# A mixture-of-experts block: the second expert's rows fetched early, and four slot tables in place of sixteen

## The chip, the cores and the metric

The kernel runs on one core of a Trainium2 chip. The metric is device time in microseconds (us), the median of the runs shown. The engines are PE (TensorE), DVE (VectorE), ACT (ScalarE), POOL (GpSimd) and SP (SyncE, which here only issues transfers). Line numbers (L1545) are those of the kernel before.

## The reference

Two transformer blocks over 512 tokens of 1024 features. The first is a sparse-attention mixer and a dense MLP; the second is differential attention with a pooling mixer, a mixture of experts, and a small gated term. The change lies in the routing of the mixture of experts:

```python
logits = xt @ w_router + b_router                 # 512 tokens x 32 experts
top_vals, top_idx = lax.top_k(logits, 4)
gates = softmax(top_vals)
...
for each expert e, over the tokens that chose it:
    gt = minimum(x @ w_gate[e] + b_gate[e], 7)
    up = clip(x @ w_up[e] + b_up[e], -7, 7)
    y  = ((up + 1) * gt * sigmoid(1.702 * gt)) @ w_down[e] + b_down[e]
out[token] += gate * y
```

where `xt` is the RMS-normed residual. The 32 experts' weights are three matrices of 1024 x 1024 in float32 each, 4 MB apiece, and each is read once from HBM.

## The kernel before

**Experts.** The last half of the program goes through 32 places. A place is an expert with room for a fixed number of its tokens: 112 for the places that are not in `FEW`, 64 for those that are. The first three places (`STATIC`) are experts 0 to 2; the others are experts in the order of how many tokens chose them, so that their numbers are known only at run time. `seq` lists the work as 768 parts, a part being 128 rows of one weight matrix: gate and up of place 0, gate and up of place 1, down of place 0, gate and up of place 2, and so on. `begin[p]` is the index of the first part of place p: 0, 16, 40, 64 for the first four.

**Parts.** float32 products are made from float32r halves. `fetch` (L1539) loads two parts with one DMA of 1 MB on SP's queue (L1545) into one of ten buffers taken in turn (`units`); ACT writes the high half `whi` of a part and DVE the low half `wlo` (both L297, the helper `split`). A buffer is free for the next load when both of its parts are split. The halves go to slots of a ring of 17 tiles (14 named s0 to s13, then `x0`, `x1` and `e0`, listed at L837), two for each part, which PE frees when it has used them. `product` (L1723) multiplies a part by the place's rows: six matmuls for a place of 112 rows, four for one of 64.

**Order.** PE, DVE, ACT and POOL run their instructions of this stretch in the order in which the program lists them (`in_order`, L1987). SP's loads are issued in program order, each when its waits are over. In the main loop (L1972), turn i first fetches up to part i + 6, then runs what `put(i, ...)` has laid beside it, then does the product of part i.

**Rows.** The rows of place p are fetched from HBM by an indirect DMA that POOL issues (`gather`, L1498) into the one buffer `xg`, transposed on PE (`turn_rows`, L1793) and split (`split_rows`, into `he` for place 0 and `xe` for the others). Place 0's are fetched from `base`, the residual before the norm, and scaled by their norms in the buffer (L1655); the other places' are fetched from `normed`, the residual after the norm, which ACT's queue stores tile by tile (`store_normed`, L1404). Place 1's gather (L1970) stands behind five of the scatters below; its `turn_rows` is beside part 10 and its `split_rows` beside part 11.

**Which rows.** For places 0 and 1 (and 2, inside the loop) the list of rows comes from a one-hot matrix product (`one_hot`, `slot_products`, `tokens_of`); for place 1 this stands at L1650 to L1653, behind the work that ranks the experts (`ranks`, `places`). For the places from 3 on it comes from tables in HBM: `scatter_entries` (L1576) writes, by 16 indirect DMAs of POOL, for each of the 512 x 4 choices of a token an entry of four numbers to row `place` of a table; there is one table for each of the four token tiles and four choices, cleared beforehand. `table_slots` (L1763) loads the 16 tables by ACT's queue beside parts 24 to 27, `sum_tables` (L1772) adds them on DVE beside parts 32 and 33, and `all_slots` (L1778) beside part 34 makes the row lists. An entry of zero is an empty slot, so a sum over tables merges them.

**`lower`** is a buffer of 128 x 1024 whose rows 0 to 63 are cleared by POOL (L1474); it is used from the first place in `FEW` on.

Of the kernel before, what the change touches and what calls it, by code (L numbers as in the profile page):

```python
# [10 lines left out]
F32 = mybir.dt.float32  # L11
# [228 lines left out]
def build(tc, I, out, dbg=None, stop=None):  # L240
# [3 lines left out]
    with es:  # L244
# [558 lines left out]
        def attention(g, fill):  # L803
# [7 lines left out]
            for i in range(len(units) + AHEAD):  # L811
# [4 lines left out]
                if i in fill:  # L816
# [20 lines left out]
                  {forward - 1: [f"g{i}" for i in range(3)], mixer - 1: [f"p{i}" for i in range(5)], experts - 1: ['x0', 'x1', 'e0']}, {"g": mixer - 1, "p": mixer + 3}, mixer)  # L837
# [434 lines left out]
        tables = [dram.tile([P * NE, 4], F32, name=f"table{j}") for j in range(4 * NT)]  # L1272
# [201 lines left out]
        nc.gpsimd.memset(lower[0:P - SMALL].bitcast(F32), 0.0)  # L1474
# [8 lines left out]
        slots = {}  # L1483

# [13 lines left out]
        def gather(p, src, m, ap):  # L1498
            nc.gpsimd.indirect_dma_start(out=xg[:m], out_offset=None, in_=src, in_offset=bass.IndirectOffsetOnAxis(ap=ap, axis=0),  # L1499
                                         bounds_check=S - 1, oob_is_err=False)  # L1500
# [75 lines left out]
        def scatter_entries(js):  # L1576
            for j in js:
                nc.gpsimd.indirect_dma_start(out=tables[j], out_offset=bass.IndirectOffsetOnAxis(ap=place[:, j // 4, j % 4:j % 4 + 1], axis=0), in_=entry[:, j // 4, j % 4], in_offset=None,
                                             bounds_check=P * NE - 1, oob_is_err=False)
# [45 lines left out]
        slot_products(ptok, oh0, (1, 2, 3), 4, told)  # L1625
        weigh(2)
# [6 lines left out]
        one_hot(slot_of[:, :, 0:1], (0,), oh0)  # L1633
        slot_products(ptok, oh0, (0,), 4, told)
        pn = W["rb"][:, 2 * NT]
        for t2 in range(NT):
            nc.tensor.matmul(pn, ones, chosen[:, t2], start=t2 == 0, stop=t2 == NT - 1)
        gi0 = tokens_of(ptok, 0)

        gather(0, base, CAP, gi0)  # L1640
        norm0 = early.tile([P, 4], F32, name="norm0")[:CAP]
        nc.vector.tensor_copy(norm0, ptok[:CAP, 0:4])
        nc.vector.tensor_tensor(out=norm0[:, 3:4], in0=norm0[:, 1:2], in1=norm0[:, 2:3], op=ALU.add)
# [6 lines left out]
        oh1, ptok1 = new_one_hot(), ps_tr(1)  # L1650
        one_hot(slot_of[:, :, 1:2], range(NT), oh1)
        slot_products(ptok1, oh1, range(NT), 2, [])
        gi1 = tokens_of(ptok1, 1)  # L1653
        fetch(2)
        for cs in (slice(0, 512), slice(512, D)):  # L1655
            scale_rows(xg[:CAP, cs], xg[:CAP, cs], norm0[:, 3:4], gpre[:CAP, cs])
# [106 lines left out]
        def table_slots(q):  # L1763

            if q == 0:
                sums.extend(row_tile("tabs").rearrange("p (j f) -> p j f", j=8) for _ in range(2))
            for j in range(4 * q, 4 * q + 4):
                nc.scalar.dma_start(sums[j // 8][:, j % 8], tables[j].rearrange("(s e) c -> s (e c)", e=NE))

        sums = []  # L1770

        def sum_tables(h):  # L1772
            tab = tabs[h] = row_tile("tab")[:, :4 * NE].rearrange("p (e c) -> p e c", c=4) if h else early.tile([P, NE, 4], F32, name="tab")
            nc.vector.reduce_sum(tab.rearrange("p e c -> p (e c)"), sums[h].rearrange("p j f -> p f j"), axis=AX)
# [3 lines left out]
        def all_slots():  # L1778
            tab = tabs[0]
            nc.vector.tensor_tensor(out=tab, in0=tab, in1=tabs[1], op=ALU.add)  # L1780
# [12 lines left out]
        def turn_rows(p):  # L1793
            pts["x", p] = turned(xg, cap[p])
# [124 lines left out]
        put(11, split_rows, 1)  # L1919
        put(14, gates_by_expert)  # L1920
# [6 lines left out]
        for q in range(4):  # L1927
            put(begin[1] + 8 + q, table_slots, q)
        for h in range(2):
            put(begin[1] + 16 + h, sum_tables, h)  # L1930
# [35 lines left out]
        scatter_entries(range(15, 10, -1))  # L1966
# [3 lines left out]
        gather(1, normed, CAP, gi1)  # L1970
# [307 lines left out]
```

## Time and profile before

| | |
|---|---|
| three runs | 2075.34, 2075.75 (median) and 2076.8 us |
| profiled execution | 2073.2 us |
| its span, first to last instruction | 2071.5 us |
| PE / DVE / ACT / POOL busy | 1968.3 / 1640.3 / 1370.9 / 414.6 us |
| moved by DMA | 554.16 MB, mean 268 GB/s |
| mean granted clock of PE, in shares of full speed | 0.985 |

Busy time counts what an engine executes; a matmul that is pipelined behind another counts as busy. The times of rows are microseconds from the start of the span. The experts' stretch runs from about 920 to 1980; its first matmul on an expert's weights starts at 928.86.

### The profile page before, as it was taken

Reading aid. Unit: us, or ns where it says so; the run is one execution under the profiler, and the core shown is the slowest. Engines: PE = TensorE matmul, PEld = TensorE weight load, DVE = VectorE, ACT = ScalarE, POOL = GpSimd, SP = SyncE. Lnnn points to the kernel's source line nnn. Section 1 sums busy time; section 2 is a strip of 40 time slices with the busy share of each in tenths; the row PEclk is TensorE's granted clock in tenths of the full one; section 3 lists DMA queues with packets and bytes.
Section 4 is the critical chain, followed back from the end, with each engine's and each line's share of the span. In section 5 each row is a group of like instructions: output and inputs, shape, how many; then the busy total and the mean of one; then the engine's idle time right before and its main releaser. Section 6 shows DMA issues by size and latency. Waiting matters only on the chain. (4 is left out here: it accounts for less than half of the span.)

```text
span 2071.5 us, 28687 instructions
## 1 busy us (share of the span) xinstructions
PE 1968.3 (95%) x9675; PEld 1507.0 (73%) x9676; DVE 1640.3 (79%) x2290; ACT 1370.9 (66%) x1889; POOL 414.6 (20%) x363
## 2 busy tenths in 40 slices
PE   8999999999999888878999999999999999999968
PEld 6777779888878887666777777777667766767546
DVE  6688874223466666678999999999999999999965
ACT  5656753222355364537799988888888888888942
POOL 0100120000010334124223444322211003201122
PEclk9999999999999998989999999999999999999989
DMA  5510464233555402248999999999999999999973
GB/s 215 173 31 22 176 230 154 91 102 102 182 202 191 129 11 72 107 173 338 403 410 406 412 406 407 402 404 402 405 396 403 399 398 402 398 407 398 365 270 106
DMA packets 113158, 554.16 MB, mean 268 GB/s; under 512 B 16739, under 2 KB 25955, under 8 KB 63852
## 3 DMA queue, kind: packets, MB, share of 16 engines
q1 hardware_dynamic: 90528, 510.04, 63.6%
q10 hardware_dynamic: 15116, 25.40, 3.6%
q0 software_dynamic: 7360, 16.82, 2.4%
q8 instruction: 78, 1.28, 0.2%
q14 instruction: 76, 0.62, 0.1%
HBM read 532.62 MB, written 26.66 MB: 270 GB/s over the span
## 5 line engine op out<-in xcount | busy, mean ns | idle before, releaser
L297 DVE TENSOR_TENSOR wlo<-wraw,whi 128x1024 fp32r<-128x1024 f32 x923 | 1076.1, 1215 | 209.4 <-ACT whi L297 203.8
L297 ACT CAST whi<-wraw 128x1024 fp32r<-128x1024 f32 x923 | 923.1, 1049 | 217.2 <-PE po L327 28.0
L1715 POOL DMA_INDIRECT ybuf<-yt,si x31 | 190.6, 6150 | 453.4 <-ACT yt L1820 453.4
L326 PE MATMUL pw<-whi,xe 128*112 128x512 f32 x544 | 215.9, 397 | 0.0
L327 PE MATMUL pw<-wlo,xe 128*112 128x512 f32 x544 | 214.4, 394 | 0.1
L328 PE MATMUL pw<-whi,xe 128*112 128x512 f32 x544 | 214.0, 393 | 0.0
L1734 PE MATMUL pw<-wlo,xe 128*64 128x512 f32 x406 | 162.9, 401 | 8.6 <-DVE wlo L297 8.0
L1733 PE MATMUL pw<-whi,xe 128*128 128x512 f32 x406 | 161.3, 397 | 3.2 <-DVE xe L297 3.2
L332 POOL TENSOR_SCALAR rstd<-ss 128x1 f32<-128x1 f32 (+1 forms) x68 | 24.8, 364 | 626.9 <-DVE ss L877 387.5
L326 PE MATMUL pw<-whi,he 128*112 128x512 f32 x320 | 128.1, 400 | 0.0
L1499 POOL DMA_INDIRECT xg<-normed,gi x31 | 62.5, 2017 | 327.2 <-PE tr L1703 284.8
L327 PE MATMUL pw<-wlo,he 128*112 128x512 f32 x320 | 126.4, 395 | 0.2
L328 PE MATMUL pw<-whi,he 128*112 128x512 f32 x320 | 126.2, 394 | 0.0
L328 PEld LDWEIGHTS pw<-whi,xe 128*112 128x112 f32 x544 | 94.7, 174 | 31.6
L326 PEld LDWEIGHTS pw<-whi,xe 128*112 128x112 f32 x544 | 94.7, 174 | 31.2
L327 PEld LDWEIGHTS pw<-wlo,xe 128*112 128x112 f32 x544 | 94.8, 174 | 30.9 <-DVE wlo L297 0.7
L1733 PEld LDWEIGHTS pw<-whi,xe 128*128 128x128 f32 x406 | 76.4, 188 | 34.2 <-DVE xe L297 3.6
L1734 PEld LDWEIGHTS pw<-wlo,xe 128*64 128x64 f32 x406 | 54.5, 134 | 46.4 <-DVE wlo L297 31.1
L1733 PE MATMUL pw<-whi,he 128*128 128x512 f32 x182 | 74.1, 407 | 0.0
L1734 PE MATMUL pw<-wlo,he 128*64 128x512 f32 x182 | 72.9, 401 | 0.0
L326 PE MATMUL pa<-x2T,whi 128*128 128x512 f32 (+1 forms) x200 | 72.6, 364 | 0.1
L327 PE MATMUL pa<-x2T,whi 128*128 128x512 f32 (+1 forms) x200 | 72.6, 363 | 0.0
(617 smaller groups left out, 4212.7 us busy)
## 6 DMA issues: line engine op xcount, KB each, us to landing
wraw<-in_we_gate_dram SPq DMA_DIRECT2D x128, 1024.0 KB, 20.4
wraw<-in_we_up_dram SPq DMA_DIRECT2D x128, 1024.0 KB, 21.5
wraw<-in_we_down_dram SPq DMA_DIRECT2D x128, 1024.0 KB, 20.4
wraw<-in_w_gu_dram SPq DMA_DIRECT2D x44, 512.0 KB, 3.8
wraw<-in_w_down_dram SPq DMA_DIRECT2D x44, 512.0 KB, 4.5
wraw<-in_w_out_dram SPq DMA_DIRECT2D x24, 512.0 KB, 5.6
yb<-ybuf SPq DMA_DIRECT2D x6, 1024.0 KB, 8.7
wraw<-in_w_v_dram SPq DMA_DIRECT2D x10, 512.0 KB, 3.9
```

What stands on the lines that cost most here:

```text
L297: return nc.scalar.copy(hi, src), nc.vector.tensor_tensor(out=lo, in0=src, in1=hi.bitcast(F32), op=ALU.subtract)
L326: nc.tensor.matmul(o, a[0], b[0], start=start, stop=False)
L327: nc.tensor.matmul(o, a[0], b[1], start=False, stop=False)
L328: W["mm"] = nc.tensor.matmul(o, a[1], b[0], start=False, stop=stop)
L332: ins = nc.gpsimd.tensor_scalar(out=r[:, :w], in0=ss, scalar1=1.0 / n, scalar2=eps, op0=ALU.mult, op1=ALU.add)
L1499: nc.gpsimd.indirect_dma_start(out=xg[:m], out_offset=None, in_=src, in_offset=bass.IndirectOffsetOnAxis(ap=ap, axis=0), bounds_check=S - ...
L1715: nc.gpsimd.indirect_dma_start(out=ybuf, out_offset=bass.IndirectOffsetOnAxis(ap=ap, axis=0), in_=y_, in_offset=None, bounds_check=4 * S - ...
L1733: nc.tensor.matmul(ps[:, cs], a[:, k, 0:P], hi, start=first, stop=False)
L1734: nc.tensor.matmul(ps[:m, cs], a[:, k, 0:m], lo, start=False, stop=False)
```

## The change

Place 1's rows are fetched next to place 0's, from `base`, into a buffer of their own: `x1`, in the tile that was the ring's 17th slot (`e0`), so that the ring has 16. For that the one-hot product for place 1 is made before the ranking of the experts, in the storage of `lower`, whose clearing moves into the loop (beside part 12). Both places' rows are scaled by their norms on DVE. All 16 scatters stand together ahead of the loop, and write to four tables, one for each choice, in place of 16. The four tables are loaded by POOL's queue beside part 20, and added by one reduction beside part 26.

```diff
@@ -834,7 +834,7 @@
         stages += ["ppppr"] + ["pp"] * 6 + ["pppp", "pppprr"]
         experts = len(stages)
         open_ring("ring2", stages + ["h"] * (NE * 24), lambda u: 2 if u < experts - 1 else SPLIT_AHEAD if u >= experts else 0,
-                  {forward - 1: [f"g{i}" for i in range(3)], mixer - 1: [f"p{i}" for i in range(5)], experts - 1: ['x0', 'x1', 'e0']}, {"g": mixer - 1, "p": mixer + 3}, mixer)
+                  {forward - 1: [f"g{i}" for i in range(3)], mixer - 1: [f"p{i}" for i in range(5)], experts - 1: ['x0', 'x1']}, {"g": mixer - 1, "p": mixer + 3}, mixer)
         if stop == "mix":
             with pool("dd") as dd:
                 for n, m in (("mixA", mixA), ("mixG", mixG)):
@@ -1269,7 +1269,7 @@
         normed = dram.tile([S, D], F32, name="normed")
         ybuf = dram.tile([4 * S, D], F32, name="ybuf")
 
-        tables = [dram.tile([P * NE, 4], F32, name=f"table{j}") for j in range(4 * NT)]
+        tables = [dram.tile([P * NE, 4], F32, name=f"table{j}") for j in range(4)]
         zeros = mixq.tile([P, 4 * NE], F32, name="zeros")
         nc.gpsimd.memset(zeros, 0.0)
         for t in tables:
@@ -1471,7 +1471,8 @@
         fold = early.tile([P, SMALL], F32R, name="fold")
         nc.vector.tensor_copy(fold, ident[:, P - SMALL:P])
         lower = early.tile([P, D], F32R, name="lower")
-        nc.gpsimd.memset(lower[0:P - SMALL].bitcast(F32), 0.0)
+        x1 = W["e0"].tile([P, D], F32, name="x1")
+        nc.gpsimd.memset(x1, 0.0)
         braws = [xg[0:NE]] + [raw_tile()[0:NE] for _ in range(2)]
         for braw, n in zip(braws, ("gate", "up", "down")):
             nc.sync.dma_start(braw, I["be_" + n])
@@ -1482,6 +1483,9 @@
             nc.vector.tensor_copy(pick0[64 * q:64 * q + 64, q], eye[64 * q:64 * q + 64, 0:STATIC])
         slots = {}
 
+        def fetched(p):
+            return x1 if p == 1 else xg
+
         def one_hot(col, tiles, oh):
             n = len(tiles)
             t = slice(tiles[0], tiles[0] + n)
@@ -1496,7 +1500,7 @@
                 done.append(tt)
 
         def gather(p, src, m, ap):
-            nc.gpsimd.indirect_dma_start(out=xg[:m], out_offset=None, in_=src, in_offset=bass.IndirectOffsetOnAxis(ap=ap, axis=0),
+            nc.gpsimd.indirect_dma_start(out=fetched(p)[:m], out_offset=None, in_=src, in_offset=bass.IndirectOffsetOnAxis(ap=ap, axis=0),
                                          bounds_check=S - 1, oob_is_err=False)
 
         def tokens_of(pt, p):
@@ -1575,7 +1579,7 @@
 
         def scatter_entries(js):
             for j in js:
-                nc.gpsimd.indirect_dma_start(out=tables[j], out_offset=bass.IndirectOffsetOnAxis(ap=place[:, j // 4, j % 4:j % 4 + 1], axis=0), in_=entry[:, j // 4, j % 4], in_offset=None,
+                nc.gpsimd.indirect_dma_start(out=tables[j % 4], out_offset=bass.IndirectOffsetOnAxis(ap=place[:, j // 4, j % 4:j % 4 + 1], axis=0), in_=entry[:, j // 4, j % 4], in_offset=None,
                                              bounds_check=P * NE - 1, oob_is_err=False)
 
 
@@ -1623,6 +1627,9 @@
         oh0, ptok, told = new_one_hot(), ps_tr(0), []
         one_hot(slot_of[:, :, 0:1], (1, 2, 3), oh0)
         slot_products(ptok, oh0, (1, 2, 3), 4, told)
+        oh1, ptok1, told1 = lower[:, :NT * CAP].rearrange("p (t c) -> p t c", c=CAP), ps_tr(1), []
+        one_hot(slot_of[:, :, 1:2], (1, 2, 3), oh1)
+        slot_products(ptok1, oh1, (1, 2, 3), 4, told1)
         weigh(2)
         logits(0)
         weigh(1)
@@ -1631,29 +1638,32 @@
         choose(0)
         position(0)
         one_hot(slot_of[:, :, 0:1], (0,), oh0)
+        one_hot(slot_of[:, :, 1:2], (0,), oh1)
         slot_products(ptok, oh0, (0,), 4, told)
+        slot_products(ptok1, oh1, (0,), 4, told1)
         pn = W["rb"][:, 2 * NT]
         for t2 in range(NT):
             nc.tensor.matmul(pn, ones, chosen[:, t2], start=t2 == 0, stop=t2 == NT - 1)
-        gi0 = tokens_of(ptok, 0)
-
-        gather(0, base, CAP, gi0)
-        norm0 = early.tile([P, 4], F32, name="norm0")[:CAP]
-        nc.vector.tensor_copy(norm0, ptok[:CAP, 0:4])
-        nc.vector.tensor_tensor(out=norm0[:, 3:4], in0=norm0[:, 1:2], in1=norm0[:, 2:3], op=ALU.add)
+
+        gis = [tokens_of(ptok, 0), tokens_of(ptok1, 1)]
+        norms_of = []
+        for p, pt in enumerate((ptok, ptok1)):
+            gather(p, base, CAP, gis[p])
+            t = early.tile([P, 4], F32, name=f"norm{p}")[:CAP]
+            nc.vector.tensor_copy(t, pt[:CAP, 0:4])
+            nc.vector.tensor_tensor(out=t[:, 3:4], in0=t[:, 1:2], in1=t[:, 2:3], op=ALU.add)
+            norms_of.append(t)
         weigh(0)
         nc.vector.scalar_tensor_tensor(out=keys, in0=pn, scalar=float(NE), in1=keys, op0=ALU.mult, op1=ALU.add)
         nc.vector.tensor_copy(room, pn)
         matches((0,))
         ranks()
         places()
-        oh1, ptok1 = new_one_hot(), ps_tr(1)
-        one_hot(slot_of[:, :, 1:2], range(NT), oh1)
-        slot_products(ptok1, oh1, range(NT), 2, [])
-        gi1 = tokens_of(ptok1, 1)
         fetch(2)
-        for cs in (slice(0, 512), slice(512, D)):
-            scale_rows(xg[:CAP, cs], xg[:CAP, cs], norm0[:, 3:4], gpre[:CAP, cs])
+        for p in range(2):
+            x = fetched(p)[:CAP]
+            for cs in (slice(0, 512), slice(512, D)):
+                scale_rows(x[:, cs], x[:, cs], norms_of[p][:, 3:4], gpre[:CAP, cs])
         store_normed(0)
         rp.release()
         gp.release()
@@ -1760,24 +1770,19 @@
                 cs = slice(c * 512, (c + 1) * 512)
                 W["mm"] = nc.tensor.matmul(ps[:SMALL, cs], fold, lower[:, cs], start=False, stop=True, skip_group_check=True)
 
-        def table_slots(q):
-
-            if q == 0:
-                sums.extend(row_tile("tabs").rearrange("p (j f) -> p j f", j=8) for _ in range(2))
-            for j in range(4 * q, 4 * q + 4):
-                nc.scalar.dma_start(sums[j // 8][:, j % 8], tables[j].rearrange("(s e) c -> s (e c)", e=NE))
-
-        sums = []
-
-        def sum_tables(h):
-            tab = tabs[h] = row_tile("tab")[:, :4 * NE].rearrange("p (e c) -> p e c", c=4) if h else early.tile([P, NE, 4], F32, name="tab")
-            nc.vector.reduce_sum(tab.rearrange("p e c -> p (e c)"), sums[h].rearrange("p j f -> p f j"), axis=AX)
+        def load_tables():
+            rows["tabs"] = row_tile("tabs")[:, :16 * NE].rearrange("p (j f) -> p j f", j=4)
+            for j in range(4):
+                nc.gpsimd.dma_start(rows["tabs"][:, j], tables[j].rearrange("(s e) c -> s (e c)", e=NE))
+
+        def sum_tables():
+            tab = tabs[0] = early.tile([P, NE, 4], F32, name="tab")
+            nc.vector.reduce_sum(tab.rearrange("p e c -> p (e c)"), rows.pop("tabs").rearrange("p j f -> p f j"), axis=AX)
 
         tabs = {}
 
         def all_slots():
             tab = tabs[0]
-            nc.vector.tensor_tensor(out=tab, in0=tab, in1=tabs[1], op=ALU.add)
             gi, si = rows_of(early, tab[:, :, 1], tab[:, :, 2], NE)
             for p in range(NE):
                 r, m = RANK[p], cap[p]
@@ -1791,7 +1796,7 @@
             beside[i].append(lambda: f(*a))
 
         def turn_rows(p):
-            pts["x", p] = turned(xg, cap[p])
+            pts["x", p] = turned(fetched(p), cap[p])
 
         def split_rows(p):
             operand["x", p] = halves_of(pts.pop(("x", p)), "xe" if p else "he", cap[p])
@@ -1917,6 +1922,7 @@
         put(8, picks)
         put(10, turn_rows, 1)
         put(11, split_rows, 1)
+        put(12, lambda: nc.gpsimd.memset(lower[0:P - SMALL].bitcast(F32), 0.0))
         put(14, gates_by_expert)
         put(8 + SPLIT_AHEAD + 1, order_product)
         put(8 + SPLIT_AHEAD + 2, order_end)
@@ -1924,10 +1930,8 @@
             put(16 + 2 * tt, gates_end, tt)
         put(begin[1], lambda: gather(2, normed, cap[2], rows.pop("gi2")[:cap[2]]))
         put(begin[1] + 5, rooms)
-        for q in range(4):
-            put(begin[1] + 8 + q, table_slots, q)
-        for h in range(2):
-            put(begin[1] + 16 + h, sum_tables, h)
+        put(20, load_tables)
+        put(begin[1] + 10, sum_tables)
         put(begin[1] + 18, all_slots)
         put(begin[3] + 4, turn_gates)
         put(begin[3] + 6, split_gates)
@@ -1963,12 +1967,10 @@
             else:
                 hop(d + 8, few[p], "down", p, lambda i: put(i, finish_rows, p), 1 if p == NE - 2 else SPLIT_AHEAD)
 
-        scatter_entries(range(15, 10, -1))
+        scatter_entries(range(15, -1, -1))
         keep_warm(10, bias[:, 0:P], bias[:, 0:512])
         turn_rows(0)
         split_rows(0)
-        gather(1, normed, CAP, gi1)
-        scatter_entries(range(10, -1, -1))
         for i, (n, p, k) in enumerate(seq):
             fetch(i + 1 + SPLIT_AHEAD)
             for f in beside[i]:
```

## Rows read from the trace of the kernel before

**Rows 1.** The page, its first line.
```profile
span 2071.5 us, 28687 instructions
```

**Rows 2.** Windows: PE, PEld, DVE, ACT, POOL busy us; granted clock, DMA share, GB/s.
```profile
952.00:954.00 2.00, 2.00 (x9) 1.75 (x8) 0.94 (x2) 1.42 (x3) 1.60 (x2) 0.50 1.03 427
...
964.00:988.00 24.00, 24.00 (x112) 18.20 (x111) 22.14 (x31) 16.92 (x18) 0.00 (x0) 1.00 0.76 260
...
1000.00:1400.00 400.00, 400.00 (x1842) 291.12 (x1841) 396.72 (x380) 353.83 (x393) 145.52 (x25) 1.00 1.01 406
1400.00:1960.00 560.00, 548.25 (x2461) 383.48 (x2459) 536.08 (x514) 481.97 (x534) 99.48 (x34) 1.00 1.01 401
```

**Rows 3.** SP's DMA queue, 964 to 988, 1000 to 1400: packets, MB, share.
```profile
q1 hardware_dynamic: 655, 4.80, 55.3%
...
q1 hardware_dynamic: 21452, 156.24, 96.8%
```

**Rows 4.** SP's waits, 860 to 2000: us in total, times, longest.
```profile
SPq L1545 <- DVE wlo L297: 326.4, 182, 36.1
...
SPq L1545 <- DMA tabs<-table: 17.2, 3, 10.7
```

**Rows 5.** Timeline of SP's issues, 961 to 979: start us, us, what.
```profile
961.11 0.33 SPq L1545 DMA_DIRECT2D wraw<-in_we_gate_dram  x1
...
972.17 0.33 SPq L1545 DMA_DIRECT2D wraw<-in_we_gate_dram  x1
...
978.12 1.73 SPq L1545 DMA_DIRECT2D wraw<-in_we_gate_dram  x2
```

**Rows 6.** Timeline of DVE, 920 to 990; in brackets idle before, releaser.
```profile
920.90 0.62 DVE L1488 TENSOR_TENSOR oh<-iota,slot_of 128x448 fp32r<-128x448 f32 x1
...
922.85 2.40 DVE L297 TENSOR_TENSOR wlo<-wraw,whi 128x1024 fp32r<-128x1024 f32 x2
925.17 1.40 DVE L352 SCALAR_TENSOR_TENSOR xg<-xg,norm,g_ffn_norm 112x512 f32<-112x512 f32 x2
926.50 1.27 DVE L352 SCALAR_TENSOR_TENSOR hx<-hx,rstd,g_ffn_norm 128x1024 f32<-128x1024 f32 x1
...
952.94 1.37 DVE L297 TENSOR_TENSOR xe<-tr,xe 128x448 fp32r<-128x448 f32 x2 [3.71 <-ACT xe L297]
...
961.31 2.45 DVE L297 TENSOR_TENSOR wlo<-wraw,whi 128x1024 fp32r<-128x1024 f32 x2
...
975.14 2.34 DVE L297 TENSOR_TENSOR wlo<-wraw,whi 128x1024 fp32r<-128x1024 f32 x2
...
979.20 1.23 DVE L297 TENSOR_TENSOR wlo<-wraw,whi 128x1024 fp32r<-128x1024 f32 x1 [0.65 <-ACT whi L297]
...
987.15 1.98 DVE L1774 TENSOR_REDUCE tab<-tabs 128x128 f32<-128x1024 f32 x1
```

**Rows 7.** Timeline of PE, 938 to 955.
```profile
938.87 0.52 PE L1495 MATMUL tr<-info,oh 128*112 128x2 f32 x4 [2.69 <-DVE oh L1488]
...
951.35 1.73 PE L1703 MATMUL tr<-ident,xg 112*128 112x112 f32 x8 [4.46 <-DMA xg<-normed,gi]
...
954.58 0.40 PE L327 MATMUL pw<-wlo,he 128*112 128x512 f32 x1
```

**Rows 8.** Timeline of POOL, 937 to 951.
```profile
937.10 5.93 POOL L1499 DMA_INDIRECT xg<-normed,gi  x1 [8.48 <-DVE wlo L297]
...
950.38 0.97 POOL L1578 DMA_INDIRECT table<-entry,place  x1 [0.30 <-issue]
```

**Rows 9.** Timeline of ACT, 928 to 971.
```profile
928.21 0.97 ACT L297 CAST he<-tr 128x448 fp32r<-128x448 f32 x2 [12.06 <-PE tr L1703]
...
969.75 1.78 ACTq L1768 DMA_DIRECT2D tabs<-table  x4
```

**Rows 10.** DMAs of tile table, 905 to 1000; then of one gather.
```profile
DMA to landing us min/median/max: 1.8/5.8/8.3
...
xg<-base,gi POOLq DMA_INDIRECT x1, 4.4
```

## The prediction

> **What bounds the kernel now.** I read the page first: the span is 2071.5 us [rows 1], and the profiled execution 2073.2 us, so 1.7 us lie around it; it is 2.55 us below the median of the runs, 2075.75. The sum is made against 2073.2 and moved up by 2.55 at its end.
>
> Then the windows of the experts' stretch [rows 2]. From 1000 to 1400 the DMA engines are busy without a break (share 1.01, 406 GB/s), and so is PE (400.00 of 400 us). From 1400 to 1960 the DMA engines go on as before (1.01, 401 GB/s), but PE has 560 - 548.25 = 11.75 us idle. So the flow of weights decides the end: PE first works off a backlog, then waits for data. What the flow gains before 1000 is there at the end, as long as PE can follow, and for that it has its own gain before 1000 and those 11.75 us.
>
> The flow has a hole. From 964 to 988 the share is 0.76 [rows 2]. SP's queue, which carries the weights, moved 4.80 MB there, against 156.24 MB in 400 us, or 0.3906 MB per us, in full flow [rows 3]: 4.80 / 0.3906 = 12.3 us' worth in 24 us, a hole of 11.7 us.
>
> The waits and the timelines say what makes it. Most of SP's waiting is for DVE, which frees the buffers (326.4 us), and costs nothing while earlier loads still flow. But 17.2 us in three waits end with the landing of a load of the slot tables [rows 4]. After 961.11 SP issues nothing until 972.17, then nothing until 978.12 [rows 5], though the buffer of the first of these loads was free at 961.31 + 2.45 = 963.76 [rows 6]. The table loads are issued by ACT, from 969.75 on [rows 9]. A weight load reads none of their bytes, so what SP waits for is an order, not data; the trace shows that it waits, not what ties the two. In the list of SP's waits no transfer issued by POOL stands.
>
> PE has a second loss. It sits idle for 4.46 us until place 1's rows land, and the eight transposes then take 1.73 us [rows 7] at a granted clock of 0.50, half of full speed, 1.2 of 2.4 GHz [rows 2]. The gather behind it began on POOL only at 937.10 and took 5.93 us [rows 8].
>
> **The change part by part.** *Place 1's rows early.* PE's idle time starts at 951.35 - 4.46 = 946.89; at 954.58, after eight transposes and four matmuls, it is in step again [rows 7]. At full clock these cost 1.73 / 2 = 0.87 us and 4 x 400 / 1842 = 0.87 us [rows 2, 7], so 7.69 - 1.74 = 5.95 us go. DVE loses its 3.71 us of idle time ahead of `xe` [rows 6]. The new gather is hidden: the one from `base` landed 4.4 us after issue [rows 10], and DVE scales place 0's rows only at 925.17 [rows 6].
>
> *What it adds in front.* The late one-hot product goes: DVE spent 920.90 to 922.85 on it, 1.95 us with its wait for PE [rows 6]. It comes back earlier: a comparison over four tiles (0.62 us there, somewhat more in two pieces), two more small products on PE and some four small DVE operations; I take 1.3 us. Scaling place 1's rows adds 1.40 us, ahead of the scaling of `hx` that ends at 926.50 + 1.27 = 927.77 [rows 6]. ACT's store of that tile, and behind it ACT's `he` at 928.21 [rows 9], so come 1.3 + 1.4 - 1.95 = 0.75 us later. Bounds: 0, if the early comparison falls into DVE's idle time, and 1.6 us, if the whole product counts again. The warm-up matmuls on PE, which no longer wait for the late product, run earlier, and PE may begin the experts at the low clock; a PE late by less than the 2.69 us for which it waits for DVE at 938.87 [rows 7] loses nothing. PE's gain is 5.95 - 0.75 = 5.2 us.
>
> *Table loads on POOL.* SP's 17.2 us of waits go [rows 4], and so do ACT's 16 issues, the first four of which keep its queue for 1.78 us [rows 9] and later make DVE wait (0.65 us at 979.20); of the two reductions of 1.98 us each, one over half as many values stays [rows 6]. So DVE, which gains 3.71 - 0.75 = 3.0 us at first, gains over 5 by 988.
>
> *Scatters.* POOL issued one in 0.97 us beside an idle DVE [rows 8]. With four tables the fifth writes what the first wrote, so it must wait for that one to land, 5.8 us in the median [rows 10]. From about 922, where `places` ends, 16 scatters are three such rounds of 5.8 + 1 us and four issues, some 25 us: to about 948, landed by 954. A gather and four table loads follow; at POOL's 0.97 to 5.93 us per issue [rows 8] the last is issued between 959 and 978 and lands 5.8 us later. The reduction that needs them stands beside part 26, behind the split of part 31, which DVE began at about 976.3 (the second of the pair that starts at 975.14 [rows 6]) and will begin some 3 us earlier. So DVE waits between nothing and 10 us there. I take 0 to 2, since the rows nearest to a plain transfer are the short ones; PE has some 6 us of split parts ahead of it then, so 2 us cost nothing.
>
> *One slot less.* A high half now waits for the part eight before, not nine. That binds only where DVE runs far ahead; I take nothing, and a bound of 1.4 us, a part's six matmuls at 0.23.
>
> *The sum.* When SP issues as buffers come free, five pairs are freed from 963.76 to 975.14 + 2.34 = 977.48 [rows 6], each about 3 us earlier than that. A pair is 1.049 / 0.3906 = 2.7 us of flow; three are still under way at 961, so eight last 21.5 us, to about 982.5. The next buffers come free by 978. That closes the hole but for the places where buffers are freed in bursts: I leave 2 us open. 11.7 - 2 = 9.7 us, and PE can follow: 5.2 + 11.75 is more. 2073.2 - 9.7 = 2063.5 us for an execution like the profiled one, and 2066.1 beside the median of the runs.
>
> **The rivals.** *Only PE's stall counts: 2070.6 us.* The holes at 972 and 978 may be an order that the loads keep whoever issues them, or the buffers may come free too slowly. Then the end moves by PE's 5.2 us alone, since the flow stays tied to what PE and DVE free: 2075.75 - 5.2 = 2070.55. For it: from 1000 on PE is never idle, so its 5.2 us are all that the loads' buffers can count on. Against it: the 8.4 us between a free buffer and the issue at 972.17 [rows 5, 6]. The Trainium skill, "DMA: Bandwidth & Descriptors", section "Issuing engines are not separate DMA queues", says that starting transfers from several engines saves only the issuing sequencer's time; by that rule moving the table loads would free ACT for 16 issues and nothing else, which is this rival. By that rule alone the trace is not explained: it has SP waiting for those landings [rows 4].
>
> *The table loads come late, and DVE stands: slower, 2080.9.* This is the rival on the other side. POOL's issue beside a busy DVE was 5.93 us against 0.97 beside an idle one [rows 8]. Say the loads, now behind 16 scatters and a gather, land at 994. The buffers freed before the reduction keep the flow up to about 983. The next one is freed a reduction (some 0.7 us) and two splits (2.4 us) after the landing, and a pair takes at least 2.7 us, so the flow stands until 999.8: a hole of 16.8 us where 11.7 were, 5.1 us slower, 2075.75 + 5.1. It decides from a landing at about 989 on; some us earlier the change comes out even, at about 2074. For it: the long gather. Against it: every issue would have to be as slow, and the scatters wait longer than their median too. By the Trainium skill, "DMA: Bandwidth & Descriptors", section "SWDGE vs HWDGE vs iDMA", GpSimd writes its descriptors into SBUF, where DVE can lock it out, while transfers issued from ACT or SP are immune; that rule speaks against this part of the change and for this rival, and the long gather agrees with it.
>
> **How the numbers follow.** The hole closes (gain 7 to 11.7, that is 2064 to 2068.8): 0.55. Only PE's stall counts, or half the hole (gain 4.2 to 7): 0.20. Loads late by some us, about even: 0.13. Slower: 0.12. 0.2% is 4.15 us, about what a measurement of this kernel tells from no change, so faster 0.75, within it 0.13, slower 0.12. The forecast is 2066.1. The range is 2063 to 2074: the full hole below, with a little for DVE's shorter work, and the even case above; what is left out is the slower rival and some of the even case.
>
> **What would show it.** Right: SP's waits name no table load; the DMA share from 964 to 988 is over 0.9; PE goes from part 9 to the transposes without a gap near 947; `he` on ACT at about 929; DVE's reduction starts without a wait before 980; place 2's first product about 5 us earlier. Wrong: a wait of DVE for the tables, a wait of SP for something else in the same place, or PE idle for DVE between 1000 and 1400, where now it has none.

## The result, and the profile after

The changed kernel takes 2051.44 us (median of four runs, 2048.88 to 2052.45), the kernel before 2076.12 us beside it: a ratio of 0.9884, 95% interval 0.9871 to 0.9896, or 24.7 us faster. I had forecast 9.7 us (2066.1) and a range whose lower end was 2063. The profiled execution took 2050.86 us, its span:

```profile
span 2048.9 us, 28291 instructions
```

What the change was to do in the experts' stretch, it did. The windows that answer to [rows 2], then SP's queue from 964 to 988, as in [rows 3]:

```profile
952.00:954.00 2.00, 2.00 (x10) 1.54 (x9) 2.00 (x3) 1.12 (x2) 0.39 (x1) 1.00 0.97 410
964.00:988.00 24.00, 24.00 (x114) 18.36 (x113) 23.97 (x28) 19.03 (x21) 1.00 (x1) 1.00 0.96 360
1000.00:1400.00 400.00, 400.00 (x1839) 290.65 (x1838) 394.36 (x377) 359.68 (x397) 164.13 (x25) 1.00 1.01 406
1400.00:1960.00 560.00, 550.07 (x2484) 391.18 (x2483) 543.96 (x523) 490.30 (x541) 180.48 (x35) 0.99 0.98 398
```

```profile
q1 hardware_dynamic: 1169, 8.47, 93.7%
```

The hole is closed (share 0.96 for 0.76, 8.47 MB for 4.80), and the slow clock at 952 is gone (1.00 for 0.50). SP's waits from 860 to 2000 name no table load now. Their first two rows (line numbers are those of the kernel whose trace is shown), and SP's timeline from 955 to 975:

```profile
SPq L1549 <- DVE wlo L297: 523.5, 270, 35.9
SPq L1549 <- DMA wraw<-in_we_gate_dram: 103.7, 49, 4.7
```

```profile
955.40 9.19 SPq L1549 DMA_DIRECT2D wraw<-in_we_gate_dram  x3
966.84 6.95 SPq L1549 DMA_DIRECT2D wraw<-in_we_up_dram  x3
```

Five of these six loads are issued between 960 and 975; before has two there [rows 5]. In before the first row of its waits, for buffers that DVE frees, stood at 326.4 us [rows 4], the second, for the landing of its own loads, at 191.7: now SP waits less for landings and more for buffers.

PE goes from a product straight into place 1's transposes (no bracket, so no idle time), at full clock, 0.93 us for the eight where before took 1.73 [rows 7]:

```profile
942.60 0.40 PE L328 MATMUL pw<-whi,he 128*112 128x512 f32 x1
942.84 0.93 PE L1713 MATMUL tr<-ident,x 112*128 112x112 f32 x8
```

POOL's queue went as I had laid it out, and faster than its long gather [rows 8] made me fear. The two gathers, the last of the 16 scatters, and the table loads:

```profile
911.99 1.31 POOL L1503 DMA_INDIRECT xg<-base,gi  x1 [7.09 <-DVE em L1510]
913.60 1.80 POOL L1503 DMA_INDIRECT x<-base,gi  x1 [0.30 <-DVE eqs L1562]
...
946.52 1.89 POOL L1582 DMA_INDIRECT table<-entry,place  x1 [0.31 <-DVE xe L297]
...
953.62 2.24 POOL L1776 DMA_DIRECT2D tabs<-table  x4 [2.87 <-DMA table<-entry,place]
```

DVE comes to the reduction 13 us after that and doesn't wait. Its timeline, first in front, then there:

```profile
917.69 2.36 DVE L297 TENSOR_TENSOR wlo<-wraw,whi 128x1024 fp32r<-128x1024 f32 x2
...
921.29 1.41 DVE L352 SCALAR_TENSOR_TENSOR x<-x,norm,g_ffn_norm 112x512 f32<-112x512 f32 x2
922.61 1.28 DVE L352 SCALAR_TENSOR_TENSOR hx<-hx,rstd,g_ffn_norm 128x1024 f32<-128x1024 f32 x1
...
969.00 1.11 DVE L1780 TENSOR_REDUCE tab<-tabs 128x128 f32<-128x512 f32 x1
```

But all of this stands some 5 us further left than it should. The scaling of `hx` begins at 922.61 where before has 926.50 [rows 6], with *more* work in front of it. To see where the time comes from, I followed one event, the end of DVE's split of a pair's first part, through the timelines of both kernels:

| DVE's split ends, us | pair 0 | pair 80 | pair 200 | pair 370 | last pair | per pair, 200 to 370 |
|---|---|---|---|---|---|---|
| before | 924.07 | 1155.52 | 1475.67 | 1944.64 | 1979.00 | 2.759 |
| after | 918.91 | 1145.75 | 1461.31 | 1918.98 | 1953.35 | 2.692 |
| ahead by | 5.2 | 9.8 | 14.4 | 25.7 | 25.7 | |

So there are three gains: 5 us before the first expert, 5 us in the stretch that I had studied, and 16 us after 1155, where I had expected none. The span ends 22.6 us earlier, as the work behind the last expert takes 3 us longer.

The last of the three is the largest. From 1400 on PE waits for its weights in before, and after gets them faster at nearly the same share. SP's queue from 1100 to 1900 (packets, MB, share of 16 engines), of before:

```profile
q1 hardware_dynamic: 42439, 309.05, 96.2%
```

and of after:

```profile
q1 hardware_dynamic: 43003, 313.13, 96.0%
```

A packet of this queue took 0.962 x 16 x 800 us / 42439 = 290.1 ns on average before and 285.7 ns after. The mean is over two sizes: one packet in nine has 4 bytes and takes 9 ns, and by the packed traces those of 8192 bytes took 325.2 ns before and 320.4 after. The engines were equally busy, and packets were 1.5% shorter. That is the quantity to explain.

### The profile page after: what moved, and what is told of

The parts are those of the page before. It is cut to its first block, busy times and chain, and to the rows that moved or that the text cites. A ratio compares the mean times of both kernels' runs of the same rounds, so it can differ in the third digit from the quotient of the medians.

```text
span 2048.9 us, 28291 instructions
## 1 busy us (share of the span) xinstructions
PE 1962.3 (96%) x9675; PEld 1510.6 (74%) x9676; DVE 1637.4 (80%) x2293; ACT 1375.7 (67%) x1889; POOL 517.2 (25%) x368
## 5 line engine op out<-in xcount | busy, mean ns | idle before, releaser
L1725 POOL DMA_INDIRECT ybuf<-yt,si x31 | 274.3, 8847 | 373.8 <-ACT yt L1825 373.8
L1503 POOL DMA_INDIRECT xg<-normed,gi x30 | 75.0, 2499 | 278.9 <-PE tr L1713 251.2
L328 PE MATMUL pa<-x2T,wlo 128*128 128x512 f32 (+1 forms) x200 | 72.6, 363 | 0.0
```

The costliest lines, as they stand in the source:

```text
L328: W["mm"] = nc.tensor.matmul(o, a[1], b[0], start=False, stop=stop)
L1503: nc.gpsimd.indirect_dma_start(out=fetched(p)[:m], out_offset=None, in_=src, in_offset=bass.IndirectOffsetOnAxis(ap=ap, axis=0), bounds_ch ...
L1725: nc.gpsimd.indirect_dma_start(out=ybuf, out_offset=bass.IndirectOffsetOnAxis(ap=ap, axis=0), in_=y_, in_offset=None, bounds_check=4 * S - ...
```

## The experiments

Thirteen kernels ran, on four chips, each beside the kernel before on the same chip: four kernels on each of three chips, and the last of the table alone on the fourth. The table is the overview; "ns" is the mean time of a packet of SP's queue, worked out as above from one profiled execution. Gains in the text are differences of medians; the ratio with its interval is taken over all runs and need not be their quotient.

| kernel | us | before there | ratio, 95% interval | MB, 1100 to 1900 | ns |
|---|---|---|---|---|---|
| a_16clears | 2053.72 | 2074.07 | 0.9911 (0.9890 to 0.9932) | 313.52 | 285.4 |
| b_gather | 2058.24 | 2074.07 | 0.9929 (0.9910 to 0.9948) | 314.51 | 284.8 |
| b_tables | 2071.57 | 2074.07 | 0.9983 (0.9972 to 0.9994) | 309.03 | 290.5 |
| a_act_loads | 2051.45 | 2074.07 | 0.9890 (0.9872 to 0.9908) | 313.98 | 285.3 |
| b_pad32 | 2062.85 | 2074.90 | 0.9946 (0.9925 to 0.9967) | 312.32 | 286.8 |
| a_pad32 | 2062.54 | 2074.90 | 0.9941 (0.9923 to 0.9959) | 309.50 | 289.4 |
| b_pad160 | 2072.08 | 2074.90 | 0.9986 (0.9976 to 0.9996) | 309.87 | 289.4 |
| a_all10 | 2049.46 | 2074.90 | 0.9883 (0.9862 to 0.9903) | 313.82 | 285.5 |
| a_again | 2051.64 | 2074.09 | 0.9896 (0.9879 to 0.9912) | 313.50 | 285.4 |
| a_1bigclear | 2052.02 | 2074.09 | 0.9894 (0.9877 to 0.9912) | 313.53 | 285.7 |
| b_all10 | 2058.98 | 2074.09 | 0.9931 (0.9915 to 0.9947) | 314.99 | 284.7 |
| a_best | 2048.38 | 2074.09 | 0.9876 (0.9858 to 0.9893) | 313.87 | 285.4 |
| b_gather_pad32 | 2069.82 | 2073.64 | 0.9983 (0.9973 to 0.9992) | 309.63 | 289.6 |

**Half a change at a time.** b_gather and b_tables are the two halves of the diff, each on the kernel before. b_gather, shown as an edit of the changed kernel, from which it takes the tables' half back:

```diff
-        tables = [dram.tile(..., name=f"table{j}") for j in range(4)]
+        tables = [dram.tile(..., name=f"table{j}") for j in range(4 * NT)]   # and loads by ACT, as before
```

> The kernel before with the early rows of place 1 alone (own buffer, sixteen slots, scaled on chip, all scatters ahead of the loop); tables, clears and table loads as before, sixteen each, loaded by ACT. Theory 1: PE's stall of 5 us goes, but the hole in the flow stays (about 11 us from 964 to 988), and so do the clears; PE runs ahead by 5 us until the flow binds, at about 1430, and the end moves by nothing to 5 us: 2071 to 2076. Rival, the buffer or the ring of sixteen makes the later flow faster: 2056 to 2061, with the pace from 1450 to 1900 at 2.70 us a pair where before has 2.77.

b_tables:

```diff
+        tables = [dram.tile(..., name=f"table{j}") for j in range(4)]
...
+                nc.gpsimd.dma_start(rows["tabs"][:, j], ...)
```

> The kernel before with the tables' part alone: four tables, so four clears, loaded by POOL and added by one reduction; place 1's rows late as before and seventeen slots. Theory 1: the front's 5 us and the hole's 10 us are gained, the stall of PE (6 us) stays: the flow is ahead by 10 to 15 us at 1100 and the end comes at 2061 to 2066, with the later pace at 2.77 us a pair. Rival, fewer and smaller transfers are what makes the later flow faster, or a flow that is ahead stays faster: 2051 to 2056.

Theory 1 lost on both, and so did the rival on the second. The rival on the first had the time right and, as the unused tiles show below, the cause wrong. b_tables closes the hole, as its window shows, while PE keeps its stall, as its waits show:

```profile
964.00:988.00 24.00, 24.00 (x109) 18.12 (x108) 23.83 (x34) 16.89 (x18) 2.25 (x4) 1.00 0.94 344
```

```profile
PE tr L1703 <- DMA xg<-normed,gi: 5.0, 1, 5.0
```

It gained 2.5 us, and pair 80 is split at 1155.91, no earlier than before. Most of what the closed hole brought is given back by 1030. The two windows behind the hole, of before and then of b_tables:

```profile
988.00:1000.00 12.00, 12.00 (x58) 9.12 (x56) 11.93 (x15) 9.95 (x11) 1.27 (x2) 1.00 1.02 415
1000.00:1030.00 30.00, 30.00 (x140) 22.65 (x139) 30.00 (x30) 23.67 (x27) 9.57 (x2) 1.00 1.00 405
```

```profile
988.00:1000.00 12.00, 12.00 (x58) 9.24 (x57) 11.96 (x15) 9.94 (x11) 1.00 (x1) 1.00 0.89 331
1000.00:1030.00 30.00, 30.00 (x141) 22.57 (x140) 27.77 (x27) 23.46 (x26) 3.70 (x2) 1.00 0.98 385
```

The DMA engines moved 2.0 MB more than before from 964 to 988 (344 for 260 GB/s), and 1.6 MB less from there to 1030. By the packed trace each load there is issued 0.03 us after DVE has freed its buffer, and PE, late by its stall, sets when that is.

b_gather gained 15.8 us, and most of it late: pair 80 at 1154.59 (0.9 us ahead), the last pair at 1960.11 (18.9 ahead), and packets of 284.8 ns. Whatever makes a packet shorter came with the early rows' half of the diff.

**The queue of the table loads.**

```diff
-                nc.gpsimd.dma_start(rows["tabs"][:, j], tables[j]...)
+                nc.scalar.dma_start(rows["tabs"][:, j], tables[j]...)
```

> The changed kernel with its four table loads issued by ACT in place of POOL, at the same place. Theory 1, SP's loads wait for whatever ACT has under way: a hole of some 2 to 4 us opens where four loads and not sixteen stand, so 2053 to 2056, and SP's waits name the tables again. Rival, sixteen loads were the trouble and not the queue: 2051, SP's waits name no table load.

Neither quite: SP's waits name the tables again, with a third of the time of [rows 4], and the end doesn't move (2051.45).

```profile
SPq L1549 <- DMA tabs<-table: 5.5, 3, 3.0
```

Four loads on ACT hold SP for 5.5 us, which its ten buffers bridge; on POOL they hold it for nothing. With four loads the issuing engine thus shows in SP's waits and not in the time. Sixteen loads on POOL were not run.

What ties SP to those landings, which the prediction left open, stands in the programs as built. The transfers of SP and ACT together use eight landing semaphores, and a transfer waits until the one that last used its semaphore has landed; POOL's use eight others. In before the three weight loads that the hole holds up longest wait in this way for `table1`, `table5` and `table8`. It is an order of the program, not of the chip.

**The clears.** Sixteen tables had to be cleared, by one transfer each on SP's queue, at 671 to 686. The prediction has no word on their becoming four. The timeline of ACT, before:

```profile
678.34 0.34 ACTq L1310 DMA_DIRECT2D rcol<-in_col_ffn_norm_dram  x1
682.20 0.34 ACTq L348 DMA_DIRECT2D g_b_router<-in_b_router_dram  x1
682.57 1.07 ACT L297 CAST x3T<-tr 128x512 fp32r<-128x512 f32 x2 [5.98 <-DMA rcol<-in_col_ffn_norm_dram]
```

and after:

```profile
677.10 0.91 ACTq L1310 DMA_DIRECT2D rcol<-in_col_ffn_norm_dram  x1
678.05 0.73 ACTq L348 DMA_DIRECT2D g_b_router<-in_b_router_dram  x1
679.29 1.25 ACT L297 CAST x3T<-tr 128x512 fp32r<-128x512 f32 x2 [2.51 <-PE tr L360]
```

ACT's cast waits behind ACT's loads, and those stand still for 3.9 us while SP sends clears. a_16clears gives the changed kernel twelve spare clears, a_1bigclear their bytes in one transfer:

```diff
+        spare = [dram.tile([P * NE, 4], F32, name=f"spare{j}") for j in range(12)]
-        for t in tables:
+        for t in tables + spare:
```

> The changed kernel with twelve spare tables beside its four, cleared by twelve more transfers on SP's queue, as the kernel before cleared sixteen. Theory 1, the clears cost time in front: in the trace of before ACT issues one load at 678.34 and the next only at 682.20, and its cast behind them comes at 682.57, against 679.29 after; the shift is 4.8 us when the experts' first weights are issued (867.50 against 862.66). By it this run issues those weights about 5 us later than the changed kernel does, and ends about 5 us later, at 2056. Rival, the front is hidden by the flow of weights: 2051, unchanged. Second rival, the place of the tables in HBM sets the later pace of the flow, of which this run has sixteen again: then it gives back the 15 us that the changed kernel gains between 1400 and 1950 as well, 2071.

```diff
+        spare = dram.tile([12, P * NE, 4], F32, name="spare")
+        nc.sync.dma_start(spare..., zeros[:, None].to_broadcast([P, 12, 4 * NE]))
```

> The changed kernel with the bytes of twelve more clears written by one more transfer on SP's queue. Twelve transfers of their own cost about 2.3 us at the end (2053.72 against 2051.45 of a kernel with four, on one chip), and about 3 us at ACT's first cast behind them. Theory 1, what costs is the number of transfers, since SP's and ACT's loads wait for one another's landings in turn: one more transfer costs nothing or below 1 us, 2051 to 2052. Rival, the 0.79 MB are what costs: 2053 to 2054.

With twelve more clears the load of `b_router` is issued at 682.82 again and the cast begins at 683.20; with the same bytes in one transfer they stand at 678.46 and 679.67:

```profile
682.82 0.34 ACTq L348 DMA_DIRECT2D g_b_router<-in_b_router_dram  x1
683.20 1.07 ACT L297 CAST x3T<-tr 128x512 fp32r<-128x512 f32 x2 [5.58 <-DMA rcol<-in_col_ffn_norm_dram]
```

```profile
678.46 1.17 ACTq L348 DMA_DIRECT2D g_b_router<-in_b_router_dram  x1
679.67 1.07 ACT L297 CAST x3T<-tr 128x512 fp32r<-128x512 f32 x2 [2.74 <-PE tr L360]
```

So it is the number of transfers, and again the eight semaphores: in the program of before the load of `b_router` waits for the landing of the seventh clear, in that of after for no clear. At the end the twelve cost 2.3 us by medians, half of what theory 1 had (2053.72 against a_act_loads on the same chip), but those intervals overlap, so a cost at the end is not shown. The rival of the tables' place in HBM is out: with sixteen tables again the packets stay short (285.4 ns). The 4.8 us that the two first profiles differ by in front (867.50 and 862.66 for the second pair's load) were partly chance: over all profiles it is 864.5 to 867.6 with sixteen clears and 862.7 to 866.2 with four.

**The placement.** The seven weight buffers `E0` to `E6` lie in each partition behind the pool that holds `xg`. In the programs as built they start at byte 132832 before and 132864 after, and go on in steps of 8192: the change puts one more small tile into that pool, the norms of place 1 (`norm1`), and pushes them 32 bytes on, to a multiple of 256. An unused tile of 32 bytes does the same to the kernel before; in the changed one it pushes the buffers on to 32 bytes past the multiple:

```diff
+        early.tile([P, 8], F32, name="pad")      # b_pad32, a_pad32; [P, 40] in b_pad160
         xg = early.tile([P, D], F32, name="xg")
```

> The kernel before with one unused tile of 32 bytes per partition in the pool of xg, nothing else. In the built program of before, the seven weight buffers E0 to E6 start at byte 132832 of each partition and every 8192 bytes from there, 32 bytes short of a multiple of 256; in the changed kernel the small tile norm1 pushes them to 132864, a multiple of 256. The pad does the same to before. New theory, the start of the buffers in SBUF sets the time of a weight packet: 1100 to 1900 moves 1.3% more (some 313 MB on SP's queue, where before moved 309), a pair takes 2.70 us and not 2.77 once the flow binds, and the end comes some 14 us earlier, at about 2060. Rival, the ring of sixteen slots or the early rows did it: 2074, unchanged, 309 MB.

> The changed kernel with the same unused 32 bytes, so that the seven buffers start 32 bytes past a multiple of 256: the change without its accident of placement. New theory: PE keeps its 10 us until the flow binds, the flow then takes 2.77 us a pair again, and the end comes at 2062 to 2068 (what is left is the front's 5 us and what the flow gained by 988, 5 MB or 13 us, less 1 MB given back by 1100). Rival, placement does nothing: 2051.

> The kernel before with 160 unused bytes, so that the seven buffers start at 132992, a multiple of 128 but not of 256. The Trainium skill, DMA: Bandwidth & Descriptors, section How a descriptor splits into AXI transactions, says that a transaction must start at a multiple of 256 bytes and that a descriptor that does not start there costs one more. By that rule this run is as slow as before: 2074, 309 MB from 1100 to 1900. Rival, a multiple of 64 or 128 is enough: 2060, 313 MB.

These three decide it. An unused tile of 32 bytes makes the kernel before 12 us faster (packets of 286.8 ns), and takes 11 to 12 of the change's 24.7 us away (289.4 ns). At a multiple of 128 alone a packet is nearly as long as before (289.4 for 290.1 ns), and the kernel 2.8 us faster, where the multiple of 256 gave 12. Over all the kernels the packet times fall into two groups that don't meet: 284.7 to 286.8 ns with the seven at a multiple of 256, 289.4 to 290.5 without. The tile also moves the small tiles behind `xg`; no run moves the seven buffers alone, but it is the weights' packets that change. SP's queue in b_pad32 and in a_pad32:

```profile
q1 hardware_dynamic: 42887, 312.32, 96.1%
```

```profile
q1 hardware_dynamic: 42502, 309.50, 96.1%
```

The Trainium skill, "DMA: Bandwidth & Descriptors", section "How a descriptor splits into AXI transactions", has the boundary of 256 bytes: a transaction must start at a multiple of it, and in its example 576 bytes take four transactions off the boundary for three on it. The page says this of reads; what moved here is the side that is written. If it holds there too, an 8192-byte packet off the boundary takes 33 transactions for 32, 3% more, an estimate from the page. The runs agree on the boundary: 32 bytes short of it, 32 and 128 past it are all slow. In size they show less: 8192-byte packets took 325.2 ns in before and 319.1 with all ten buffers at a multiple (b_all10, below), 1.9%. They don't show why a packet takes longer, only that it does.

The other three buffers (`y0` to `y2`) start 32 bytes short in both kernels. a_all10 and b_all10 move them too:

```diff
         ep = alloc("ep", side="right")
+        ep.tile([P, 56], F32, name="pad")
```

> The changed kernel with 224 unused bytes in the pool beside the other three weight buffers (y0 to y2), which start 32 bytes short of a multiple of 256 in both kernels; with them all ten start at one. New theory, three of ten buffers still pay: seven gave about 1.3% of the flow, so three more give 0.5%, some 5 us of the 820 us between 1100 and 1920 as far as the flow binds, which in the changed kernel it does only from about 1500 on: 2 to 5 us, 2046 to 2049. Rival, the three do nothing more or PE is the bound: 2051.

> The kernel before with 32 unused bytes ahead of the seven weight buffers and 224 ahead of the other three, so that all ten start at a multiple of 256. The seven alone gave 12 us (2062.85 against 2074.90). If each buffer counts alike, ten give up to 12 x 10 / 7 = 17 us where the flow binds: 2058. Rival, the three count for nothing, or PE is the bound from there on: 2062 to 2063.

On the kernel before ten buffers give 15.1 us where seven gave 12.1 (284.7 ns; 10/7 of 12.1 would be 17.2); the two intervals overlap. In the changed kernel the three give 2 us by medians at most, inside the intervals: there PE, busy for 798.1 of the 800 us from 1100 to 1900, is nearer to being the bound.

**The early rows without the shift.** b_gather with the 32 unused bytes:

```diff
+        early.tile([P, 8], F32, name="pad")      # on b_gather
```

> The early rows of place 1 alone, with 32 unused bytes more, so that the seven buffers start 32 past a multiple of 256: that part without the placement that came with it. Theory: each of the two parts alone leaves the other's loss standing. The table loads open the hole as before, PE, 5 us ahead at 983, runs dry behind it, and little is left: PE's pace from 1100 to 1400 within 1 us of before, the end at 2071 to 2075. Rival, the parts add up: what the early rows gained over the pad alone (2058.24 against 2062.85 on another chip, each some 12 to 16 us below before) is theirs: 2069 to 2070.

3.8 us, 0.9983 (0.9973 to 0.9992). The time lies in the rival's range and below the theory's, and the interval of the gain, 1.7 to 5.6 us, holds both: the time doesn't decide between them. The trace shows the theory's course. Of the windows 964 to 988 and 988 to 1000, and of SP's waits:

```profile
964.00:988.00 24.00, 24.00 (x115) 18.36 (x114) 20.18 (x27) 16.97 (x20) 0.00 (x0) 1.00 0.87 323
988.00:1000.00 12.00, 9.80 (x40) 7.03 (x39) 11.93 (x16) 7.95 (x10) 2.08 (x2) 0.86 0.91 315
```

```profile
SPq L1550 <- DMA tabs<-table: 16.4, 3, 7.9
```

The hole stays, and PE, no longer held up at 947, runs dry behind it, between 988 and 1000: 2.2 us idle and a mean granted clock of 0.86 (0.50 from 996 to 998, after the idle time). It begins place 2's transposes 7.4 us ahead of before (980.2 against 987.6) and place 3's 3.0 us ahead (1020.5 against 1023.5), little more than the 2.5 us by which it had started early (first split at 921.54).

**All together.** a_best is a_all10 with the four clears issued 190 us later, behind the experts' biases; a_again is the changed kernel beside it.

```diff
-        for t in tables:
-            nc.sync.dma_start(t..., zeros)
...
+        bloads = [nc.sync.dma_start(braw, I["be_" + n]) for braw, n in zip(braws, ("gate", "up", "down"))]
+        for t in tables:
+            hold(nc.sync.dma_start(t..., zeros), bloads[0])
```

> The changed kernel with all ten weight buffers at a multiple of 256 and its four clears moved behind the biases of the experts on SP's queue, about 190 us later. Theory 1: ACT's loads at 671 to 678 wait for no clear, which gives 0 to 2 us in front beside the changed kernel, and the three buffers give 0 to 2: 2047 to 2051. Rival, the clears beside the experts' first loads delay those: 2052 to 2054.

> The changed kernel once more, to stand beside the other three on the same chip: 2051 by every theory. Its front varies, too: in the two profiles of kernels with the same clears the experts' first weights (the second pair) were issued at 862.66 and 866.19.

2048.38 against 2051.64: the fastest kernel of the study by its median, 25.7 us below before, though its interval overlaps that of the changed kernel.

## Why the prediction was wrong

**The step that failed** is the one that carries the sum to the end: "What the flow gains before 1000 is there at the end, as long as PE can follow", with the share of 1.01 [rows 2] read as a flow that can't go faster, so that the pace after 1000 is the same in both kernels and no term stands for it. A share says that packets are under way all the time, not how long one takes. At one and the same share of 96%, SP's queue moved 309 MB in 800 us with the buffers 32 bytes off and 312 to 315 MB with them at a multiple of 256. The change moved them by accident, and no term of my sum looked at where a new tile goes. That is worth 11 to 12 us, by a_pad32 and by b_pad32, with intervals of some 4 us to either side: about half of the 24.7. Why such a packet takes longer stays open.

**The sum without it** came out nearly right. a_pad32 is the change without the better placement: 12.4 us faster (8.5 to 16.0 by its interval), where I had 9.7. A term that was left out is the twelve clears, 2.3 us at the end by medians, which is not clear of the noise; with it the sum is 12.0. The agreement may in part be luck: in the profiled execution of a_pad32 the first split ends 2.9 us ahead of before, earlier than anything that the sum counts, and the second pair's load varies by as much between kernels with the same clears.

**The parts don't add up**, by medians. The early rows alone gave 3.8 us, the tables' part alone 2.5, both together 12.4 (the intervals of the sum, 3 to 11, and of the whole, 8.5 to 16.0, overlap, so the times alone don't show it). The traces show how more can be gained by both: from 1000 to 1400 PE is never idle, so only PE's lead counts there, and each loss hides the other. The 11.75 us that I counted as room for PE to follow lie after 1400; at 1000 the loads wait for buffers that PE's pace frees, and of the 2.0 MB that b_tables gains in the hole 0.4 MB is left at 1030. Without the stall PE runs into the hole (b_gather_pad32), and without the hole it still stands at the stall (b_tables). I had treated the two as parallel, one for the flow and one for PE; they lie one behind the other.

**The table loads.** SP's 17.2 us of waits went, as said, but that POOL issues the loads is not what the time needed: a_act_loads is as fast. The rule that the prediction weighs against the trace (the Trainium skill, "DMA: Bandwidth & Descriptors", section "Issuing engines are not separate DMA queues"), that starting transfers from several engines saves only the issuing time, agrees with the time of that run (2051.45, and 2051.64 with POOL on another chip). What it didn't explain, SP's waits for the landings, is the eight semaphores: 16.4 us with sixteen loads on ACT (b_gather_pad32), 5.5 with four, none with four on POOL.

**The small terms.** PE's gain in the stretch was to be 5.2 us: pair 80 is 9.8 us ahead, 5.2 of them from the front, so 4.6. The added work in front was to cost 0.75 us, at most 1.6: the lead falls from 5.2 at the first split to 3.9 at the scaling of `hx`, so 1.3. The last scatter was to end at about 948: 948.4. The reduction was to wait 0 to 2 us: none. `he` on ACT came at 924.30 and not at 929, by the front. The missing slot shows in ACT's waits for PE to free one, from 1000 to 1400: 12.5 us in b_tables with seventeen slots, 26.4 in after with sixteen. PE is never idle there, so it cost nothing.

**The rivals.** "Only PE's stall counts" describes the early rows' run (3.8 us where it had 5.2), and no more. The slower case, late table loads, did not come: POOL issued the four within 2.24 us at 953.62, 13 us before DVE needed them, and none of its indirect issues between 912 and 950 took over 2 us. That the long gather of 5.93 us [rows 8] would be rare is not shown: later in the same trace gathers take up to 6.2 us and scatters up to 17.4, beside a busy DVE.

## What to carry to other kernels

Before a small tile is added, look at where it pushes the buffers behind it; here 32 unused bytes in front of the load buffers were worth about as much as all of the change's scheduling. A queue with a share of 1.0 still has a rate: divide share by packets, and ask why a packet takes what it takes. When a transfer waits for one whose bytes it doesn't read, look in the built program for the semaphore that both use. When two losses follow each other on the same path, removing one shows next to nothing, and the test of the other half tells more than a sum.

## What the runs showed of the hardware

- A packet of 8192 bytes into SBUF took 319.1 to 321.6 ns on average (1100 to 1900, ten kernels) with seven or all ten of the buffers at a multiple of 256 bytes, and 324.3 to 325.5 ns (five kernels) with seven of them 32 or 128 bytes past one or 32 short of one and the other three 32 short: about 1.5% of a flow that runs for 1000 us, at one and the same DMA share of 96%.
- In these programs, by their semaphores and not by the chip, many small transfers on SP's queue hold up ACT's loads: with sixteen clears of 64 KB ACT issues nothing for 3.5 to 4.2 us and casts about 3 us later; twelve of them as one transfer of the same bytes cost nothing there. Sixteen table loads issued by ACT held SP for 16 to 17 us and four for 5.5; there number and bytes fell together.
